# A row sum over 67 MB: blocks of 16 rows in place of 8, rows shared evenly between two engines, and a last block cut 8, 5, 2 and a split row

## The chip, the cores and the metric

The kernel runs on one core of a Trainium2 chip. The metric is device time in microseconds (us) of one execution; the time before is the median of 13 runs, 164.68 us (164.46 to 165.12).

## The reference

```
batch, seq, dim = 32, 512, 1024          # x: float32
def reference(x, multiplier):            # multiplier = 0.5
    return (np.sum(x, axis=-1) * multiplier).astype(np.float32)
```

Each of 16,384 rows of 1024 numbers is summed and multiplied by 0.5. 67.1 MB are read and 64 KiB written.

## The kernel before

The rows are laid over the 128 partitions so that partition p has rows 128 p to 128 p + 127, one after another in memory. So each partition has 128 rows of 4 KiB, and a load of c rows for all partitions moves 128 contiguous pieces of c x 4 KiB.

Fifteen big blocks (lines 74 to 91) of 8 rows each are loaded into a pool of three buffers (line 76; 4 MiB a load, in pieces of 32 KiB). VectorE sums 7 of the 8 rows with one reduce (line 78) and multiplies the 7 sums (line 83). ScalarE does the eighth with an activation that copies, scales and accumulates (line 53, called from line 90); it writes its scaled copy over the row, and a second small instruction reads the accumulator out.

The last 8 rows of each partition, the taper (lines 93 to 103), are loaded in six pieces of 2, 2, 1, 1, 1 and 1 rows, into buffers of their own (line 97). ScalarE does the first five rows; VectorE does the last three with `tensor_tensor_reduce` (line 62), which adds the two halves of a row to each other and accumulates, so that 1024 numbers take 512 steps. It too is followed by a small accumulator read.

All loads and the one store at the end (line 106) are issued by SP, in program order. A load into a buffer that is used again waits until both engines have done with it and until the load before it landed. The taper's loads don't wait for a buffer. The store waits for the last results of both engines. The names in the profile are `x_tile_b` for the big blocks, `x_tile_s` for the taper, `staging` for unscaled sums and `out_sbuf` for results.

Of the kernel before, what the change touches and what calls it, by code (L numbers as in the profile page):

```python
# [1 line left out]

# [4 lines left out]


@with_exitstack  # L10
def kernel(
    ctx: ExitStack,
    tc: tile.TileContext,
    x: bass.AP,
    multiplier: float,
    out: bass.AP,
):
    nc = tc.nc
    P = nc.NUM_PARTITIONS
    fp32 = mybir.dt.float32  # L20

    x_flat = x.flatten_outer_dims()
    N, D = x_flat.shape
    H = D // 2
    out_flat = out.rearrange("b s -> (b s)")

    assert N % P == 0
    rows_per_part = N // P

    taper = [(2, "s"), (2, "s"), (1, "s"), (1, "v"), (1, "v"), (1, "v")]  # L30
    taper_rows = sum(sz for sz, _ in taper)
    big_rows = 8
    assert (rows_per_part - taper_rows) % big_rows == 0
    n_big = (rows_per_part - taper_rows) // big_rows

    scalar_rows_per_big = 1
    vec_rows_per_big = big_rows - scalar_rows_per_big

    x_rows = x_flat.rearrange("(p c) d -> p c d", p=P)
    out_view = out_flat.rearrange("(p c) -> p c", p=P)  # L40

    big_pool = ctx.enter_context(tc.tile_pool(name="big", bufs=3))
    small_pool = ctx.enter_context(tc.tile_pool(name="small", bufs=4))
    res_pool = ctx.enter_context(tc.tile_pool(name="res", bufs=1))
    small_bufs = {2: 2, 1: 4}

    staging = res_pool.tile([P, rows_per_part], fp32)
    out_sbuf = res_pool.tile([P, rows_per_part], fp32)

    mul = float(multiplier)  # L50

    def scalar_row_sum(x_tile, r, col):
        nc.scalar.activation(  # L53
            out=x_tile[:, r, :],
            in_=x_tile[:, r, :],
            func=mybir.ActivationFunctionType.Copy,
            scale=mul,
            accum_out=out_sbuf[:, col : col + 1],
        )

    def vector_row_sum(x_tile, r, col):
        nc.vector.tensor_tensor_reduce(  # L62
            out=x_tile[:, r, 0:H],
            in0=x_tile[:, r, 0:H],
            in1=x_tile[:, r, H:D],
            scale=mul,
            scalar=0.0,
            op0=mybir.AluOpType.add,
            op1=mybir.AluOpType.add,
            accum_out=out_sbuf[:, col : col + 1],  # L70
        )

    c0 = 0
    for _ in range(n_big):
        x_tile = big_pool.tile([P, big_rows, D], fp32, name="x_tile_b")
        nc.sync.dma_start(out=x_tile, in_=x_rows[:, c0 : c0 + big_rows, :])  # L76

        nc.vector.reduce_sum(  # L78
            out=staging[:, c0 : c0 + vec_rows_per_big],
            in_=x_tile[:, 0:vec_rows_per_big, :],  # L80
            axis=mybir.AxisListType.X,
        )
        nc.vector.tensor_single_scalar(  # L83
            out=out_sbuf[:, c0 : c0 + vec_rows_per_big],
            in_=staging[:, c0 : c0 + vec_rows_per_big],
            scalar=mul,
            op=mybir.AluOpType.mult,
        )
        for r in range(vec_rows_per_big, big_rows):
            scalar_row_sum(x_tile, r, c0 + r)  # L90
        c0 += big_rows

    for sz, eng in taper:
        x_tile = small_pool.tile(
            [P, sz, D], fp32, name=f"x_tile_s{sz}", tag=f"s{sz}", bufs=small_bufs[sz]
        )
        nc.sync.dma_start(out=x_tile, in_=x_rows[:, c0 : c0 + sz, :])  # L97
        for r in range(sz):
            if eng == "s":
                scalar_row_sum(x_tile, r, c0 + r)  # L100
            else:
                vector_row_sum(x_tile, r, c0 + r)
        c0 += sz
    assert c0 == rows_per_part

    nc.sync.dma_start(out=out_view, in_=out_sbuf)


# [1 line left out]
_INS = ['x', 'multiplier']  # L110
_OUTS = [((32, 512), 'float32')]
#: Inputs that are plain numbers.
_NUMBERS = {'multiplier': 0.5}


# [26 lines left out]
```

## Time and profile before

| | |
|---|---|
| Median of 13 runs | 164.68 us |
| Profiled execution, its own time | 164.63 us |
| Its span, first to last instruction | 162.6 us |
| VectorE (DVE) busy | 118.9 us, 73% |
| ScalarE (ACT) busy | 23.9 us, 15% |
| DMA queue, share of 16 engines' span | 96.7% |
| Mean rate over the span | 413 GB/s |
| Big load, from issue to landing | 21.4 us (median) |
| Reduce of 7 rows (L78) | 7.62 us, 15 times |
| ScalarE row (L53) | 1.06 us, and 0.19 for the accumulator |
| VectorE row in the taper (L62) | 0.69 us, and 0.08 for the accumulator |

The profile is of one execution. DVE is VectorE, ACT ScalarE, SPq the queue of SP, which issues the DMAs. In the timeline a row gives start, duration, engine, line and operation, then what is written and read, and in brackets the idle time of the engine before it and what ended that. The row of 40 slices gives tenths of busy share; in the table of stretches each row has the busy time of VectorE, ScalarE and GpSimd, then the granted clock of TensorE, the share of the DMA engines' time and the rate.

### The profile page before, as it was taken

How to read it: one execution, taken by the hardware profiler on the slowest of the kernel's cores; microseconds unless marked ns; L12 is line 12 of the kernel's file. 1: busy time of each engine (PE TensorE's matmuls, PEld its weight loads, DVE VectorE, ACT ScalarE, POOL GpSimd, SP SyncE). 2: the span in 40 equal slices, each digit the busy share in tenths (PEclk: the TensorE clock that was granted, in tenths of full speed). 3: DMA queues.
4: the chain of work that ended last, by engine and by line, in shares of the span. 5: the costliest groups of instructions: out<-in, count | busy, mean ns of one | idle time of the engine just before them, and what ended most of it. 6: DMA issues, size and time to landing. Idle time of an engine off the chain costs nothing.

```text
span 162.6 us, 170 instructions
## 1 busy us (share of the span) xinstructions
DVE 118.9 (73%) x36; ACT 23.9 (15%) x41; POOL 0.2 (0%) x4
## 2 busy tenths in 40 slices
DVE  0007959599595977959599695968959598695982
ACT  3002020020201102020020202002020020202670
POOL 0000000000000000000000000000000000000000
DMA  6999999999999999999999999999999999998990
GB/s 210 435 403 451 435 443 411 435 443 435 411 443 435 411 459 443 395 459 435 403 451 435 435 419 435 443 427 419 443 435 411 443 435 411 451 443 365 411 389 20
DMA packets 3168, 67.18 MB, mean 413 GB/s; under 512 B 352, under 2 KB 480, under 8 KB 992
## 3 DMA queue, kind: packets, MB, share of 16 engines
q1 hardware_dynamic: 3168, 67.18, 96.7%
HBM read 67.11 MB, written 0.07 MB: 413 GB/s over the span
## 4 chain that ended last, share of the span: by engine, by line
DMA 76%; DVE 19%; SPq 2%; issue 0%; DVEq 0%
DMA x_tile_b<-in_x_dram 59%; DVE staging L78 19%; DMA x_tile_s<-in_x_dram 18%; SPq L97 1%; SPq L76 1%; DVE x_tile_s L62 0%; DVEq L137 0%
## 5 line engine op out<-in xcount | busy, mean ns | idle before, releaser
L78 DVE TENSOR_REDUCE staging<-x_tile_b 128x7 f32<-128x7168 f32 x15 | 114.3, 7619 | 39.8 <-DMA x_tile_b<-in_x_dram 39.8
L53 ACT ACTIVATE x_tile_b<-x_tile_b 128x1024 f32<-128x1024 f32 x15 | 15.8, 1057 | 131.3 <-DMA x_tile_b<-in_x_dram 131.3
L53 ACT ACTIVATE x_tile_s<-x_tile_s 128x1024 f32<-128x1024 f32 x5 | 5.2, 1047 | 1.6 <-DMA x_tile_s<-in_x_dram 1.6
L83 DVE TENSOR_SCALAR out_sbuf<-staging 128x7 f32<-128x7 f32 x15 | 2.6, 171 | 0.5
L53 ACT ACTIVATION_READ_ACCUMULATOR x_tile_b<-x_tile_b 128x1 f32 x15 | 2.8, 186 | 0.0
L62 DVE CUSTOM_DVE_ANT_0 x_tile_s<-x_tile_s 128x512 f32<-128x512 f32 x3 | 2.1, 690 | 0.9 <-DMA x_tile_s<-in_x_dram 0.9
L53 ACT ACT_TABLE_LOAD x1 | 1.3, 1283 | 0.7 <-PEq L123 0.7
L53 ACT ACTIVATION_READ_ACCUMULATOR x_tile_s<-x_tile_s 128x1 f32 x5 | 0.9, 187 | 0.0
L62 DVE DVE_READ_ACCUMULATOR2_ANT out_sbuf<- 128x1 f32 x3 | 0.2, 82 | 0.0
L123 POOL MEMSET const-bfloat16-1.0<- 128x1 bf16 x1 | 0.1, 102 | 0.0
L123 POOL MEMSET const-uint8-127<- 128x1 uint8 x1 | 0.1, 101 | 0.0
L123 POOL MEMSET const-float32-0.0<- 128x1 f32 x1 | 0.1, 99 | 0.2 <-issue 0.2
L123 POOL MEMSET const-float32-1.0<- 128x1 f32 x1 | 0.1, 98 | 0.0
## 6 DMA issues: line engine op xcount, KB each, us to landing
x_tile_b<-in_x_dram SPq DMA_DIRECT2D x15, 4096.0 KB, 21.4
x_tile_s<-in_x_dram SPq DMA_DIRECT2D x2, 1024.0 KB, 24.6
x_tile_s<-in_x_dram SPq DMA_DIRECT2D x4, 512.0 KB, 27.6
out_dram<-out_sbuf SPq DMA_DIRECT2D x1, 64.0 KB, 1.5
```

Of the source, the lines that this page charges most:

```text
L53: nc.scalar.activation(out=x_tile[:, r, :], in_=x_tile[:, r, :], func=mybir.ActivationFunctionType.Copy, scale=mul, accum_out=out_sbuf[:, ...
L62: nc.vector.tensor_tensor_reduce(out=x_tile[:, r, 0:H], in0=x_tile[:, r, 0:H], in1=x_tile[:, r, H:D], scale=mul, scalar=0.0, op0=mybir.Alu ...
L76: nc.sync.dma_start(out=x_tile, in_=x_rows[:, c0 : c0 + big_rows, :])
L78: nc.vector.reduce_sum(out=staging[:, c0 : c0 + vec_rows_per_big], in_=x_tile[:, 0:vec_rows_per_big, :], axis=mybir.AxisListType.X,)
L83: nc.vector.tensor_single_scalar(out=out_sbuf[:, c0 : c0 + vec_rows_per_big], in_=staging[:, c0 : c0 + vec_rows_per_big], scalar=mul, op=m ...
L97: nc.sync.dma_start(out=x_tile, in_=x_rows[:, c0 : c0 + sz, :])
L123: nc = _bacc.Bacc("TRN2", target_bir_lowering=False, num_devices=1)
```

## The change

The loop now goes over blocks of 16 rows: seven of them in one load each (8 MiB, in contiguous pieces of 64 KiB), three buffers as before. VectorE reduces and scales rows 0 to 7, ScalarE does rows 8 to 15. The eighth block is loaded into one buffer of the same pool in five loads: rows 0 to 7, rows 8 to 12, rows 13 and 14, then columns 0 to 639 of row 15, then its columns 640 to 1023. There ScalarE does rows 4 to 7, 11, 12 and 14; VectorE does the others a row at a time by adding halves. The last row takes two VectorE instructions: the first leaves a scaled sum of 640 columns in `part`, the second starts its accumulation from `part` and adds the 384 others. SP issues 13 DMAs in place of 22. The instructions that scale and sum are of the same kinds as before. Line numbers in the changed kernel: big load 71, reduce 73, multiply 76, ScalarE row 47, VectorE row 57, the last block's loads 90 and 92, store 104.

```diff
-    taper = [(2, "s"), (2, "s"), (1, "s"), (1, "v"), (1, "v"), (1, "v")]
-    big_rows = 8
-    big_pool = ctx.enter_context(tc.tile_pool(name="big", bufs=3))
-    small_pool = ctx.enter_context(tc.tile_pool(name="small", bufs=4))
+    B = 16
+    x_pool = ctx.enter_context(tc.tile_pool(name="x", bufs=3))
+    part = res_pool.tile([P, 1], fp32, name="part")
...
+    def dve_span(t, r, lo, hi, dst, start=0.0):
+        mid = (lo + hi) // 2
+        nc.vector.tensor_tensor_reduce(
+            out=t[:, r, lo:mid],
+            in0=t[:, r, lo:mid],
+            in1=t[:, r, mid:hi],
+            scale=mul,
+            scalar=start,
+            op0=ADD,
+            op1=ADD,
+            accum_out=dst,
+        )
...
-    for _ in range(n_big):
-        x_tile = big_pool.tile([P, big_rows, D], fp32, name="x_tile_b")
-        nc.sync.dma_start(out=x_tile, in_=x_rows[:, c0 : c0 + big_rows, :])
+    for b in range(n_blocks - 1):
+        c0 = b * B
+        t = x_pool.tile([P, B, D], fp32, name="xb")
+        nc.sync.dma_start(out=t, in_=x_rows[:, c0 : c0 + B, :])
+        h = B // 2
         nc.vector.reduce_sum(
+            out=sums[:, c0 : c0 + h], in_=t[:, 0:h, :], axis=mybir.AxisListType.X
         )
...
+        for r in range(h, B):
+            act_row(t, r, c0 + r)
...
-    for sz, eng in taper:
...
-        nc.sync.dma_start(out=x_tile, in_=x_rows[:, c0 : c0 + sz, :])
+    c0 = (n_blocks - 1) * B
+    t = x_pool.tile([P, B, D], fp32, name="xb")
+    cut = 640
+    pieces = [(0, 8), (8, 13), (13, 15)]
+    for lo, hi in pieces:
+        nc.sync.dma_start(out=t[:, lo:hi, :], in_=x_rows[:, c0 + lo : c0 + hi, :])
+    for lo, hi in ((0, cut), (cut, D)):
+        nc.sync.dma_start(
+            out=t[:, B - 1, lo:hi], in_=x_rows[:, c0 + B - 1, lo:hi]
+        )
+    on_act = {4, 5, 6, 7, 11, 12, 14}
+    for r in range(B - 1):
+        if r in on_act:
+            act_row(t, r, c0 + r)
+        else:
+            dve_span(t, r, 0, D, res[:, c0 + r : c0 + r + 1])
+    dve_span(t, B - 1, 0, cut, part)
+    dve_span(t, B - 1, cut, D, res[:, rows - 1 : rows], start=part)
```

More of the change, by code (lines that the diff above doesn't have):

```diff
@@ L5 @@
 import concourse.tile as tile
-from concourse import bass_utils, mybir
+from concourse import mybir
 from concourse._compat import with_exitstack
@@ L20 @@
     fp32 = mybir.dt.float32
+    ADD = mybir.AluOpType.add
     x_flat = x.flatten_outer_dims()
     N, D = x_flat.shape
[L24 to L28, printed above, removed]
-    taper = [(2, "s"), (2, "s"), (1, "s"), (1, "v"), (1, "v"), (1, "v")]
-    taper_rows = sum(sz for sz, _ in taper)
-    big_rows = 8
-    assert (rows_per_part - taper_rows) % big_rows == 0
-    n_big = (rows_per_part - taper_rows) // big_rows
-    scalar_rows_per_big = 1
@@ L37 @@
-    vec_rows_per_big = big_rows - scalar_rows_per_big
-    x_rows = x_flat.rearrange("(p c) d -> p c d", p=P)
-    out_view = out_flat.rearrange("(p c) -> p c", p=P)
-    big_pool = ctx.enter_context(tc.tile_pool(name="big", bufs=3))
-    small_pool = ctx.enter_context(tc.tile_pool(name="small", bufs=4))
-    res_pool = ctx.enter_context(tc.tile_pool(name="res", bufs=1))
-    small_bufs = {2: 2, 1: 4}
-    staging = res_pool.tile([P, rows_per_part], fp32)
-    out_sbuf = res_pool.tile([P, rows_per_part], fp32)
@@ L50 @@
-    mul = float(multiplier)
-    def scalar_row_sum(x_tile, r, col):
+    rows = N // P
+    x_rows = x_flat.rearrange("(p c) d -> p c d", p=P)
+    out_view = out.rearrange("b s -> (b s)").rearrange("(p c) -> p c", p=P)
+    mul = float(multiplier)
+    B = 16
+    n_blocks = rows // B
+    assert N == P * rows and rows == n_blocks * B
+    x_pool = ctx.enter_context(tc.tile_pool(name="x", bufs=3))
+    res_pool = ctx.enter_context(tc.tile_pool(name="res", bufs=1))
+    sums = res_pool.tile([P, rows], fp32, name="sums")
@@ L53, in scalar_row_sum, with act_row @@
+    res = res_pool.tile([P, rows], fp32, name="res")
+    part = res_pool.tile([P, 1], fp32, name="part")
+    def act_row(t, r, col):
         nc.scalar.activation(
-            out=x_tile[:, r, :],
-            in_=x_tile[:, r, :],
+            out=t[:, r, :],
+            in_=t[:, r, :],
             func=mybir.ActivationFunctionType.Copy,
             scale=mul,
-            accum_out=out_sbuf[:, col : col + 1],
+            accum_out=res[:, col : col + 1],
         )
-    def vector_row_sum(x_tile, r, col):
+    def dve_span(t, r, lo, hi, dst, start=0.0):
+        mid = (lo + hi) // 2
@@ L62, in vector_row_sum @@
         nc.vector.tensor_tensor_reduce(
-            out=x_tile[:, r, 0:H],
-            in0=x_tile[:, r, 0:H],
-            in1=x_tile[:, r, H:D],
+            out=t[:, r, lo:mid],
+            in0=t[:, r, lo:mid],
+            in1=t[:, r, mid:hi],
             scale=mul,
[L67 to L70, printed above, removed]
-        )
-    c0 = 0
-    for _ in range(n_big):
-        x_tile = big_pool.tile([P, big_rows, D], fp32, name="x_tile_b")
-        nc.sync.dma_start(out=x_tile, in_=x_rows[:, c0 : c0 + big_rows, :])
+            scalar=start,
@@ L78 @@
+            op0=ADD,
+            op1=ADD,
+            accum_out=dst,
+        )
+    for b in range(n_blocks - 1):
[3 more added lines that the diff above has]
+        h = B // 2
         nc.vector.reduce_sum(
-            out=staging[:, c0 : c0 + vec_rows_per_big],
-            in_=x_tile[:, 0:vec_rows_per_big, :],
-            axis=mybir.AxisListType.X,
+            out=sums[:, c0 : c0 + h], in_=t[:, 0:h, :], axis=mybir.AxisListType.X
@@ L82 @@
         )
         nc.vector.tensor_single_scalar(
-            out=out_sbuf[:, c0 : c0 + vec_rows_per_big],
-            in_=staging[:, c0 : c0 + vec_rows_per_big],
+            out=res[:, c0 : c0 + h],
+            in_=sums[:, c0 : c0 + h],
             scalar=mul,
@@ L88 @@
         )
-        for r in range(vec_rows_per_big, big_rows):
-            scalar_row_sum(x_tile, r, c0 + r)
-        c0 += big_rows
-    for sz, eng in taper:
-        x_tile = small_pool.tile(
-            [P, sz, D], fp32, name=f"x_tile_s{sz}", tag=f"s{sz}", bufs=small_bufs[sz]
-        )
-        nc.sync.dma_start(out=x_tile, in_=x_rows[:, c0 : c0 + sz, :])
[L98 to L106, printed above, removed]
+        for r in range(h, B):
[9 more added lines that the diff above has]
+            out=t[:, B - 1, lo:hi], in_=x_rows[:, c0 + B - 1, lo:hi]
+        )
+    on_act = {4, 5, 6, 7, 11, 12, 14}
[6 more added lines that the diff above has]
+    dve_span(t, B - 1, cut, D, res[:, rows - 1 : rows], start=part)
+    nc.sync.dma_start(out=out_view, in_=res)
 _INS = ['x', 'multiplier']
```

## The prediction

> **What bounds the kernel now.** I read the page first (engine shares, the 40 slices, the chain), then the engines by stretches, then the SP queue's waits, then the timeline, mostly its end. From the page:
>
> ```profile
> DVE 118.9 (73%) x36; ACT 23.9 (15%) x41; POOL 0.2 (0%) x4
> DMA  6999999999999999999999999999999999998990
> q1 hardware_dynamic: 3168, 67.18, 96.7%
> DMA 76%; DVE 19%; SPq 2%; issue 0%; DVEq 0%
> ```
>
> The second row is the mean busy share of the 16 DMA engines: nines from the second slice to the last but two. No compute engine is near that. The chain gives VectorE 19%, which looks like a compute bound; the stretches (us from:to, length, engines' busy us, granted clock, DMA share, GB/s) and the SP queue's waits say otherwise:
>
> ```profile
> 32.00:62.00 30.00, 23.49 (x7) 3.49 (x7) 0.00 (x0) 1.00 1.01 434
> ...
> 130.00:150.00 20.00, 16.14 (x5) 2.85 (x5) 0.00 (x0) 1.00 0.98 421
> 150.00:158.00 8.00, 7.69 (x4) 5.94 (x12) 0.00 (x0) 1.00 1.00 408
> 158.00:160.00 2.00, 1.35 (x4) 0.00 (x0) 0.00 (x0) 1.00 0.20 78
> ```
> ```profile
> SPq L76 <- DVE staging L78: 121.5, 12, 18.9
> ```
>
> The DMA share is 0.98 to 1.01 up to 158 us. SP does wait for VectorE to free a buffer (twelve times, 121.5 us), but each time the rest of one load (1.9 us of it) and a whole further one are still queued, so the DMA engines never run dry. VectorE's 19% of the chain is how the chain is followed back through a wait that costs nothing. So the time is: start, 67.1 MB streamed without a gap, and what follows the last landing. The timeline has all three parts (start us, us, engine and line; engines start 0.02 us after a landing, so starts in which the engine had been idle are landings):
>
> ```profile
> 13.32 7.62 DVE L78 TENSOR_REDUCE staging<-x_tile_b 128x7 f32<-128x7168 f32 x1 [13.32 <-DMA x_tile_b<-in_x_dram]
> ...
> 149.30 7.62 DVE L78 TENSOR_REDUCE staging<-x_tile_b 128x7 f32<-128x7168 f32 x1 [1.90 <-DMA x_tile_b<-in_x_dram]
> ...
> 151.78 1.06 ACT L53 ACTIVATE x_tile_s<-x_tile_s 128x1024 f32<-128x1024 f32 x1 [1.25 <-DMA x_tile_s<-in_x_dram]
> ...
> 154.28 1.06 ACT L53 ACTIVATE x_tile_s<-x_tile_s 128x1024 f32<-128x1024 f32 x1 [0.31 <-DMA x_tile_s<-in_x_dram]
> ...
> 156.95 0.17 DVE L83 TENSOR_SCALAR out_sbuf<-staging 128x7 f32<-128x7 f32 x1
> ...
> 159.35 0.69 DVE L62 CUSTOM_DVE_ANT_0 x_tile_s<-x_tile_s 128x512 f32<-128x512 f32 x1 [0.53 <-DMA x_tile_s<-in_x_dram]
> 159.97 0.08 DVE L62 DVE_READ_ACCUMULATOR2_ANT out_sbuf<- 128x1 f32 x1
> 160.12 0.35 SPq L106 DMA_DIRECT2D out_dram<-out_sbuf  x1
> ```
>
> First landing at 13.30, last at 159.33; then one row on VectorE (0.69), the store's issue at 160.12, the end at 162.6. The profiled execution took 164.63, so 2.03 lies around its span; it stands 0.05 below the median of 164.68.
>
> **The stream: what a row of each length costs.** A load of 128 rows gives each of 16 engines 8 rows. Spacing of landings by row length: 32 KiB rows (4 MiB), (149.30 - 13.32)/14 = 9.713 us; 8 KiB rows (1 MiB), 2.48 and 2.50; 4 KiB rows (512 KiB), (159.35 - 154.28)/4 = 1.268. A line through the first and last: (9.713 - 1.268)/28 = 0.3016 us per KiB of row, and 1.268 - 4 x 0.3016 = 0.061 us fixed per load of eight rows an engine, some 8 ns a row. At 8 KiB it gives 2.474 against 2.49 seen, so it holds inside its span. 64 KiB lies outside it.
>
> Loads of 16 rows replace two of 8. By the line one takes 0.061 + 64 x 0.3016 = 19.365 against 2 x 9.713 = 19.426: 0.061 saved, times 7 = 0.43 us. Bounds: nothing, if a 64 KiB row goes as two of 32 KiB; a loss, if it is cut finer (below). No row shows a 64 KiB transfer. The Trainium skill, "DMA: Bandwidth & Descriptors", section "Why a DMA increments its semaphore by 16 and not by 1", says that one descriptor moves one contiguous run, and speaks of cutting only for rows longer than 64 KiB; 64 KiB is just not longer. I take 0.43.
>
> The last 8 rows of each partition: before 2 x 2.49 + 4 x 1.268 = 10.05 us (six loads). After, loads of 5 rows (20 KiB: 0.061 + 6.032 = 6.093), 2 rows (2.49), 640 columns (2.5 KiB: 0.815) and 384 columns (1.5 KiB: 0.513), 9.91 us in sum; the 8 rows before them are one load of 32 KiB rows as now. Saved 0.14. The last landing moves from 159.33 by 0.43 + 0.14 to 158.76.
>
> A rule speaks against those pieces. The same page, section "Anatomy of one DMA", gives each DMA of GpSimd's path about 2.0 us plus bytes/436e9. Read as a time per load in a row, the 320 and 192 KiB pieces would take 2.75 and 2.45 us in place of 0.815 and 0.513: 3.9 us later. The trace's own row for the nearest size (512 KiB, SP's queue) is 1.268 us of spacing, against 3.2 by the rule: with loads queued, the fixed part lies under the transfer before it. I take the row. For the same reason nine loads fewer (22 DMAs to 13) don't save nine times 2.0 us.
>
> **After the last landing.** Now: 0.69 us of VectorE. For shorter pieces I have 7168 elements in 7.619 us and 7 in 0.171: 1.040 ns an element and 0.164 fixed, which gives 0.696 for 512 against 0.693 seen. The 640-column piece (320 elements) then takes 0.497 and the last (192) 0.364. Sequence: the 2-row piece lands at 157.43; row 13 runs on VectorE 157.45 to 158.14. The 640 columns land at 158.25, run 158.27 to 158.77. The last columns land at 158.76; their instruction takes the partial sum as its start value, so it waits also for VectorE's own result: the nearest row is the multiply behind each reduce, which follows it by 0.03. Start 158.81, end 159.17, store issued 0.07 later at 159.24 instead of 160.12. Bounds of that new wait: none (0.03 less), or some 0.1 more if the per-partition start value is slow to read; only the store queues behind it. ScalarE's row 14 runs 157.45 to 158.7 (1.06 and 0.19), inside VectorE's time. The store is unchanged.
>
> **What is moved and hidden.** Per block VectorE gets 8 rows: 0.164 + 8192 x 1.040 = 8.68 plus 0.17; ScalarE 8 rows at 1.06 = 8.5 plus 0.19, against 1 before. Both lie in a block's 19.4 us. The block before the last lands 9.71 us before the 8-row piece, so both engines are through (8.9) just before they get it; if that cover were gone, the 8-row piece's four rows each (4.2 us) would still end before the 5-row piece, 6.1 later. These rows cost nothing. Buffers: the fourth load waits for block 0's release, about 9 us after it landed, with 10.5 us of one load and a whole one still queued; the last block's five issues (about 0.43 each, by the tail's present issues) stand some 30 us before their data's turn. SP queues nothing else behind them but the store. Would ScalarE's 63 rows slow the loads? In 150 to 158 ScalarE is busy 74% and the DMA share stays 1.00; its 408 GB/s is the short rows. I take nothing; a per-mille of the stream (0.15) is a fair upper bound. The start: issue and first transfer are unchanged, and no engine has been near late since.
>
> Sum on the profiled execution: 0.43 + 0.14 + (159.35 + 0.69 - 159.33) less (159.17 - 158.76), that is 0.57 + 0.71 - 0.41 = 0.87, near the 0.88 of the store's issue; 164.63 - 0.88 = 163.75, on the median 163.8.
>
> **Rivals.** *64 KiB rows go as two of 32 KiB.* Then 0.43 comes back: 164.24, say 164.2. For: 32 KiB is the longest row shown. Against: the page's words. *Rows are cut finer (slower).* Place: each of seven big loads; price: cut into 4 KiB, 16 x 1.268 - 19.426 = 0.86 each, 6.0 in all, so 170.2. Cut into 16 KiB, 4 x (0.061 + 16 x 0.3016) = 19.55, 0.12 each, 0.87 in all: 165.1; against the remaining 0.45 of gain it decides from pieces of 16 KiB downwards. Against: the page's count, 3168 packets, leaves 2176 once those under 8 KiB (992) are off; 15 x 128 rows of 32 KiB plus 2 x 128 of 8 KiB is 2176. So rows to 32 KiB are not cut. *Small last loads pay their fixed time*: 163.8 + 3.9 = 167.7. *Part of the end is given back* (a slow start value, a few tenths of disturbance by ScalarE's traffic or by a longer program): 164.1 to 164.4.
>
> **How the numbers follow.** Forecast 0.60 (163.5 to 164.1). Two of 32 KiB 0.17. Given back 0.15, half of it within 0.2% of now. Finer cut 0.05, fixed time at the end 0.03. A change within 0.2% (0.33 us, so above 164.35) can't be told from none. Faster: 0.60 + 0.17 + about 0.08 = 0.85; same 0.07; slower 0.08. The range reaches to the two-of-32 case and part of what is given back: 163.4 to 164.5.
>
> **What would show it.** Spacing of block landings: 19.37 (right), 19.43 (two of 32 KiB), above 19.5 (cut finer). Packets: 7 x 128 + 128 x 5 for the loads, plus semaphores and store, if 64 KiB goes as one. Landings of the last pieces 0.8 and 0.5 us apart; the last VectorE instruction 0.36 us, starting within 0.06 of the last landing; store issue near 159.24. The prediction is wrong if the DMA share falls under 1.00 between blocks, if the last VectorE instruction starts long after its data, or if the stream slows while ScalarE works.

## The result, and the profile after

The changed kernel takes 163.92 us (median of 11 runs, 163.66 to 164.35) against 164.63 us before (49 runs): a ratio of 0.9955, 95% interval 0.9946 to 0.9964. Forecast were 163.8 us and a range of 163.4 to 164.5. The sum holds; the terms behind it hold only in part. The profiled execution took 163.94 us with a span of 162.155 us; before, 164.63 and 162.601.

From the page of the changed kernel, the rows shown of before and the new row of the queue that loads programs:

```profile
DVE 68.1 (42%) x34; ACT 67.9 (42%) x127; POOL 0.2 (0%) x4
DMA  7979979969979979979999998998998997999990
DMA packets 1874, 67.18 MB, mean 414 GB/s; under 512 B 209, under 2 KB 465, under 8 KB 593
q1 hardware_dynamic: 1872, 67.18, 96.4%
q14 instruction: 2, 0.01, 0.0%
DMA 85%; DVE 11%; SPq 1%; issue 0%; DVEq 0%
```

1872 packets are 896 of 64 KiB (seven loads of 128 rows), 640 for the five last loads, 208 semaphore writes and 128 of the store: a 64 KiB row goes as one. In the packet records one takes 2418 ns, and one of 32 KiB 1213 to 1214. The views count a packet whole where it begins, so with packets of 2.4 us the digits of slices of 4.05 us swing (`7979`), and the shares of stretches with them:

```profile
32.00:62.00 30.00, 8.95 (x3) 8.52 (x17) 0.00 (x0) 1.00 1.00 433
...
120.00:140.00 20.00, 9.45 (x3) 8.94 (x17) 0.00 (x0) 1.00 0.96 415
140.00:150.00 10.00, 9.02 (x5) 8.70 (x17) 0.00 (x0) 1.00 0.97 419
150.00:158.00 8.00, 3.98 (x13) 5.95 (x13) 0.00 (x0) 1.00 0.96 402
158.00:160.00 2.00, 1.35 (x6) 0.88 (x2) 0.00 (x0) 1.00 0.05 18
```

From 120 to 158 us the rows show 0.96 and 0.97, and the prediction named a share under 1.00 as a sign of being wrong. With every packet cut at the edges of the stretch, the packet records give 1.00 for the first two and at least 0.99 for the third: the DMA engines stay busy, as before.

SP's wait for a buffer is there four times in place of twelve for the big loads, and again costs nothing:

```profile
SPq L71 <- DVE sums L73: 86.8, 4, 29.6
```

The timeline, first blocks and end (a reduce starts 0.02 to 0.03 behind its block's landing):

```profile
22.96 8.69 DVE L73 TENSOR_REDUCE sums<-xb 128x8 f32<-128x8192 f32 x1 [22.96 <-DMA xb<-in_x_dram]
...
42.54 8.69 DVE L73 TENSOR_REDUCE sums<-xb 128x8 f32<-128x8192 f32 x1 [10.69 <-DMA xb<-in_x_dram]
...
139.41 8.69 DVE L73 TENSOR_REDUCE sums<-xb 128x8 f32<-128x8192 f32 x1 [10.46 <-DMA xb<-in_x_dram]
...
157.73 0.69 DVE L57 CUSTOM_DVE_ANT_0 xb<-xb 128x512 f32<-128x512 f32 x1 [0.57 <-DMA xb<-in_x_dram]
...
158.52 0.49 DVE L57 CUSTOM_DVE_ANT_0 xb<-xb 128x320 f32<-128x320 f32 x1
...
158.94 0.08 DVE L57 DVE_READ_ACCUMULATOR2_ANT part<- 128x1 f32 x1
159.10 0.42 DVE L57 CUSTOM_DVE_ANT_0 xb<-xb,part 128x192 f32<-128x192 f32 x1
...
159.60 0.35 SPq L104 DMA_DIRECT2D out_dram<-res  x1
```

The first block lands at 22.93, as the prediction's line has it (13.30 + 9.71 - 0.06 = 22.95). The next reduce starts at 42.54: 19.58 for the second block, where 19.37 was forecast. The last data lands at 158.97 by the trace's landing records, the last instruction starts 0.13 later, and takes 0.42 where 0.36 was reckoned. The store is issued at 159.60, not at 159.24. So the span alone gives 0.45 us of the forecast 0.88. What makes up for it lies outside the span: 164.63 - 162.60 = 2.03 us before, 163.94 - 162.155 = 1.78 now. That was in no step of the prediction.

### The profile page after: what moved, and what is told of

Read it like the earlier page. It is cut to its first block, busy times and chain, and to the rows that moved or that the text cites. A ratio compares the mean times of both kernels' runs of the same rounds, so it can differ in the third digit from the quotient of the medians.

```text
span 162.2 us, 233 instructions
## 1 busy us (share of the span) xinstructions
DVE 68.1 (42%) x34; ACT 67.9 (42%) x127; POOL 0.2 (0%) x4
## 3 DMA queue, kind: packets, MB, share of 16 engines
q1 hardware_dynamic: 1872, 67.18, 96.4%
## 4 chain that ended last, share of the span: by engine, by line
DMA 85%; DVE 11%; SPq 1%; issue 0%; DVEq 0%
DMA xb<-in_x_dram 85%; DVE sums L73 11%; SPq L90 1%; DVE xb L57 1%; SPq L71 0%; DVE part L57 0%; DVEq L135 0%
## 5 line engine op out<-in xcount | busy, mean ns | idle before, releaser
L47 ACT ACTIVATE xb<-xb 128x1024 f32<-128x1024 f32 x63 | 65.6, 1043 | 90.3 <-DMA xb<-in_x_dram 90.3
L73 DVE TENSOR_REDUCE sums<-xb 128x8 f32<-128x8192 f32 x7 | 60.8, 8686 | 86.1 <-DMA xb<-in_x_dram 86.1
L47 ACT ACTIVATION_READ_ACCUMULATOR xb<-xb 128x1 f32 x63 | 11.8, 188 | 0.0
L57 DVE CUSTOM_DVE_ANT_0 xb<-xb 128x512 f32<-128x512 f32 (+1 forms) x9 | 5.6, 667 | 5.1 <-DMA xb<-in_x_dram 5.0
L76 DVE TENSOR_SCALAR res<-sums 128x8 f32<-128x8 f32 x7 | 1.2, 171 | 0.2
L57 DVE DVE_READ_ACCUMULATOR2_ANT res<- 128x1 f32 x9 | 0.7, 82 | 0.0
```

The lines of the kernel that those rows point to most:

```text
L47: nc.scalar.activation(out=t[:, r, :], in_=t[:, r, :], func=mybir.ActivationFunctionType.Copy, scale=mul, accum_out=res[:, col : col + 1],)
L57: nc.vector.tensor_tensor_reduce(out=t[:, r, lo:mid], in0=t[:, r, lo:mid], in1=t[:, r, mid:hi], scale=mul, scalar=start, op0=ADD, op1=ADD, ...
L73: nc.vector.reduce_sum(out=sums[:, c0 : c0 + h], in_=t[:, 0:h, :], axis=mybir.AxisListType.X)
L76: nc.vector.tensor_single_scalar(out=res[:, c0 : c0 + h], in_=sums[:, c0 : c0 + h], scalar=mul, op=mybir.AluOpType.mult,)
```

## The experiments

My theory at this point: the stream's gain is the fixed 8 ns of a row, halved in number, less what a disturbance took; the new end's gain is the shorter last instruction less a wait. The rivals: all of the gain is in the end; all of it is in the stream. "Landing" below is by the landing records; "around" is an execution's time less its span. For executions other than the profiled one the span is on record to 0.1 us only, so a single "around" of theirs is good to 0.05.

**Half of the change: the big blocks alone.**

```diff
-    pieces = [(0, 8), (8, 13), (13, 15)]
+    pieces = [(0, 8), (8, 10), (10, 12), (12, 13), (13, 14), (14, 15), (15, 16)]
...
-    for lo, hi in ((0, cut), (cut, D)):
-        nc.sync.dma_start(
-            out=t[:, B - 1, lo:hi], in_=x_rows[:, c0 + B - 1, lo:hi]
-        )
-    on_act = {4, 5, 6, 7, 11, 12, 14}
+    on_act = {4, 5, 6, 7, 8, 9, 10, 11, 12}
...
-    dve_span(t, B - 1, 0, cut, part)
-    dve_span(t, B - 1, cut, D, res[:, rows - 1 : rows], start=part)
+    dve_span(t, B - 1, 0, D, res[:, rows - 1 : rows])
```

> Half of the change: seven loads of 64 KiB rows, rows shared 8 and 8, but the last 8 rows in six loads (2, 2, 1, 1, 1, 1) and the last row whole, as before. My theory (the rows' fixed 8 ns is the gain of the stream, 0.43 us, of which a disturbance and one program fetch took back up to 0.3): block landings 19.35 to 19.37 us apart, time 164.2 to 164.5. Rival (all of the gain is in the end; the stream gains nothing net): 164.6, as before. Rival (the stream is the whole gain and the new end gives nothing): 163.9.

Measured: 164.01 us (163.82 to 164.07), ratio 0.9954 (0.9941 to 0.9968). The end of its timeline:

```profile
158.87 0.69 DVE L57 CUSTOM_DVE_ANT_0 xb<-xb 128x512 f32<-128x512 f32 x1 [0.52 <-DMA xb<-in_x_dram]
...
159.63 0.35 SPq L99 DMA_DIRECT2D out_dram<-res  x1
```

Blocks land 19.33 to 19.36 us apart, but for one of 19.43. The last landing is at 158.84 (0.49 before that of the kernel before), the time around the span is 1.77. The time is 0.2 below the theory's interval: the big blocks bring nearly all of the gain, and 0.25 of it is around the span, where the theory had nothing.

**The other half: the new end alone.** Fourteen blocks of 8 rows from a pool of three, then the last block of the change.

```diff
-    x_pool = ctx.enter_context(tc.tile_pool(name="x", bufs=3))
+    x_pool = ctx.enter_context(tc.tile_pool(name="x", bufs=1))
+    s_pool = ctx.enter_context(tc.tile_pool(name="s", bufs=3))
...
-    for b in range(n_blocks - 1):
-        c0 = b * B
-        t = x_pool.tile([P, B, D], fp32, name="xb")
-        nc.sync.dma_start(out=t, in_=x_rows[:, c0 : c0 + B, :])
-        h = B // 2
+    S = 8
+    for b in range((rows - B) // S):
+        c0 = b * S
+        t = s_pool.tile([P, S, D], fp32, name="x8")
+        nc.sync.dma_start(out=t, in_=x_rows[:, c0 : c0 + S, :])
+        h = S - 1
...
-        for r in range(h, B):
+        for r in range(h, S):
```

> The other half: fourteen blocks of 8 rows, shared 7 and 1 as before, then the new last block (8, 5, 2, 640 and 384 columns). My theory: 0.14 us from the last rows' transfers and some 0.14 from the shorter last instruction (0.55 from the last landing to its end in place of 0.69 and 0.02), so 164.3 to 164.4, landings 9.71 apart, no program fetch within the span. Rival (all gain is in the end): 163.9. Rival (the stream is the whole gain): 164.6.

Measured: 164.74 us (164.48 to 165.26), ratio 1.0008 (0.9996 to 1.0019): no gain at all, against 0.3 expected. Its end:

```profile
158.82 0.49 DVE L58 CUSTOM_DVE_ANT_0 xb<-xb 128x320 f32<-128x320 f32 x1
...
159.38 0.42 DVE L58 CUSTOM_DVE_ANT_0 xb<-xb,part 128x192 f32<-128x192 f32 x1
...
159.87 0.35 SPq L106 DMA_DIRECT2D out_dram<-res  x1
```

The last rows' transfers did get shorter: 9.87 us from the last 8-row landing to the last of all, 10.05 before. Three things eat that. The first block landed 0.10 later (13.40; in the kernels with 8-row loads it lands between 13.30 and 13.44). From the last landing to the store's issue it is 0.63 in place of 0.79, but from there to the end of the span 2.63 in place of 2.48. And 2.20 us lie around the span, not 2.03. The last two have nothing to do with how the last rows are summed, and became the questions of the later runs.

**Only the length of a row: the same blocks in two loads.**

```diff
-        nc.sync.dma_start(out=t, in_=x_rows[:, c0 : c0 + B, :])
+        for q in range(0, B, 8):
+            nc.sync.dma_start(
+                out=t[:, q : q + 8, :], in_=x_rows[:, c0 + q : c0 + q + 8, :]
+            )
```

> The changed kernel, but each block of 16 rows comes in two loads of 8 rows (rows of 32 KiB) into the same buffer: only the length of a row in a load changes. My theory: 0.061 us more for each of seven blocks, landings 19.42 apart, time 0.43 more than the changed kernel, 164.3. Rival (the length of the row is nothing): 163.9. If the slow packets at 27 to 30 us belong to 64 KiB rows, they are gone here, and the difference is 0.2.

Measured: 164.37 us (164.24 to 164.88), 0.45 above the changed kernel's 163.92. From its timeline, three reduces:

```profile
71.65 8.69 DVE L76 TENSOR_REDUCE sums<-xb 128x8 f32<-128x8192 f32 x1 [10.53 <-DMA xb<-in_x_dram]
91.36 8.69 DVE L76 TENSOR_REDUCE sums<-xb 128x8 f32<-128x8192 f32 x1 [10.82 <-DMA xb<-in_x_dram]
110.78 8.69 DVE L76 TENSOR_REDUCE sums<-xb 128x8 f32<-128x8192 f32 x1 [10.53 <-DMA xb<-in_x_dram]
```

16 rows take 19.42 (91.36 to 110.78), where one load takes 19.35: the 0.06 to 0.07 a block is the length of the row. The packet records have it too: two rows of 32 KiB (1213 to 1214 ns each) take some 9 ns more than one of 64 KiB (2418), and each engine has eight such pairs in a block, 0.07 us. Not all of the 0.45 belongs to the rows, though: this kernel issues 20 DMAs in place of 13, which by the last experiment below costs some 0.06 at the end of the program. That leaves about 0.39 for the rows. From 71.65 to 91.36 it is 19.71: here the packet records have an 8 KiB program fetch at 85.34 us, on the queue that the page calls q14, and the next landing came 0.28 late. One such packet takes 309 ns on one of the 16 engines. It delays the next landing in some executions and not in others; why is not shown.

**Sharing the rows.**

```diff
-        h = B // 2
+        h = B - 1
```

> The changed kernel with VectorE on 15 and ScalarE on 1 row of each of the seven blocks, so 49 ScalarE rows fewer and a shorter ScalarE program; VectorE needs 0.164 + 15360 x 1.040 ns = 16.1 us of 19.35 for a block. My theory (even sharing gives nothing, and the longer ScalarE program costs a fetch of 8 KiB in the middle of the stream, 0.09 us): no fetch within the span, and a time 0.1 less or equal, 163.8 to 163.9. Rival (ScalarE's writes slow the stream, the slow packets at 27 to 30 us): those slow packets are gone and it is 0.2 to 0.3 faster, 163.6. Rival (sharing the rows is needed): slower than the changed kernel, 164.2 or more.

Measured: 165.54 us, ratio 1.0051 (1.0036 to 1.0065), slower than before. Its timeline from the last big block on:

```profile
139.18 16.15 DVE L73 TENSOR_REDUCE sums<-xb 128x15 f32<-128x15360 f32 x1 [2.99 <-DMA xb<-in_x_dram]
155.25 0.68 DVE L57 CUSTOM_DVE_ANT_0 xb<-xb 128x512 f32<-128x512 f32 x1
...
160.64 0.08 DVE L57 DVE_READ_ACCUMULATOR2_ANT part<- 128x1 f32 x1
160.75 0.42 DVE L57 CUSTOM_DVE_ANT_0 xb<-xb,part 128x192 f32<-128x192 f32 x1
...
161.25 0.35 SPq L104 DMA_DIRECT2D out_dram<-res  x1
```

The last big reduce runs to 155.3, while the next 8 rows have been there since 148.9; VectorE then works off eight rows and a split one back to back (no idle time in brackets) until 161.17, 2.4 us behind the last landing at 158.75. I had compared 16.1 us with a block's 19.35, but behind the last big block only 9.7 pass to the next piece. My theory that sharing gives nothing falls; the prediction's paragraph had it right with its 8.9 of 9.71. The stream itself is undisturbed, with landings 19.34 to 19.36 apart, and no program fetch.

**The changed kernel again.** No edit.

> The changed kernel once more, to see which of its losses come back: the slow packets at 27 to 30 us (0.22 us on the second block's landing) and the program fetch of 8 KiB at 85 us (0.09). My theory: the fetch comes back at the same place, since it belongs to ScalarE's program; the slow packets don't, and blocks 2 to 7 all land 19.35 to 19.45 apart. Rival: both belong to the kernel and come back. Time 163.8 to 164.0.

Measured: 163.82 us (163.65 to 163.94), ratio 0.9944 (0.9931 to 0.9958). Three of its reduces:

```profile
23.25 8.69 DVE L73 TENSOR_REDUCE sums<-xb 128x8 f32<-128x8192 f32 x1 [23.25 <-DMA xb<-in_x_dram]
42.59 8.69 DVE L73 TENSOR_REDUCE sums<-xb 128x8 f32<-128x8192 f32 x1 [10.44 <-DMA xb<-in_x_dram]
...
139.34 8.69 DVE L73 TENSOR_REDUCE sums<-xb 128x8 f32<-128x8192 f32 x1 [10.46 <-DMA xb<-in_x_dram]
```

Six blocks in 116.09 us, 19.35 each; 116.45 in the first profile. The slow packets of 27 to 30 us are gone, so they do not come in every execution of this kernel. The program fetch is there again (87.1 us), this time without a cost. This execution lost 0.3 at its start instead (23.25 for 22.96).

**The last row in one piece.**

```diff
-    pieces = [(0, 8), (8, 13), (13, 15)]
+    pieces = [(0, 8), (8, 13), (13, 15), (15, 16)]
...
-    for lo, hi in ((0, cut), (cut, D)):
-        nc.sync.dma_start(
-            out=t[:, B - 1, lo:hi], in_=x_rows[:, c0 + B - 1, lo:hi]
-        )
...
-    dve_span(t, B - 1, 0, cut, part)
-    dve_span(t, B - 1, cut, D, res[:, rows - 1 : rows], start=part)
+    dve_span(t, B - 1, 0, D, res[:, rows - 1 : rows])
```

> The changed kernel with the last row in one load of 4 KiB rows and one VectorE instruction: loads 8, 5, 2, 1 rows. My theory: the last loads take 1.27 us in place of 1.26 (0.79 and 0.47), so the last landing stays within 0.05; the last instruction is 0.69 from 0.02 behind it in place of 0.42 from 0.13 behind it: 0.16 us later, time 164.0 to 164.1. Rival (the split's whole reckoned gain of 0.33 is there): 164.25. Rival (the wait and the start value eat the split's gain): 163.9.

Measured: 164.11 us (163.92 to 164.32), 0.29 above the changed kernel of the same chip's runs. Its end:

```profile
158.99 0.69 DVE L57 CUSTOM_DVE_ANT_0 xb<-xb 128x512 f32<-128x512 f32 x1 [0.53 <-DMA xb<-in_x_dram]
...
159.77 0.35 SPq L99 DMA_DIRECT2D out_dram<-res  x1
```

From the last landing (158.97) to the store 0.80, against 0.63 with the split: the split is worth 0.16, as the theory has it. Another 0.07 of the 0.29 is behind the store (2.63 in place of 2.55). The 0.06 left is within the scatter of five executions each. The profiled one also had slow packets, again at 27 to 30 us: its first blocks lay 19.49 and 19.54 apart.

**Another cut.**

```diff
-    cut = 640
+    cut = 576
```

> The changed kernel with the last row cut at 576 in place of 640 columns. My theory (the last instruction waits for the partial sum, 0.13 behind the last landing, not for its data): the second piece lands 0.55 behind the first, the first piece's instruction takes 0.46, so the partial sum is ready at about the last landing; the last instruction (224 elements) takes 0.45 and starts 0.03 to 0.06 behind the landing; the store is issued 0.04 to 0.07 earlier. In time 163.85, hardly told from 163.92. Rival (the start is late for another reason): it starts 0.13 behind the landing as before, and the store 0.03 later.

Measured: 164.04 us (163.69 to 164.09), ratio 0.9954 (0.9940 to 0.9967), not to be told from the changed kernel's 0.9944 (0.9931 to 0.9958) of the same chip's runs. The trace can tell:

```profile
158.55 0.08 DVE L57 DVE_READ_ACCUMULATOR2_ANT part<- 128x1 f32 x1
158.82 0.45 DVE L57 CUSTOM_DVE_ANT_0 xb<-xb,part 128x224 f32<-128x224 f32 x1 [0.19 <-DMA xb<-in_x_dram]
...
159.36 0.35 SPq L104 DMA_DIRECT2D out_dram<-res  x1
```

The partial sum is read out by 158.63, the data lands at 158.69, and still the instruction starts at 158.82, 0.13 behind the landing as with 640. My explanation (it waits for the partial sum) falls, the rival holds: landing to store 0.67 in place of 0.63.

**No start value.**

```diff
-    dve_span(t, B - 1, cut, D, res[:, rows - 1 : rows], start=part)
+    dve_span(t, B - 1, cut, D, res[:, rows - 1 : rows])
```

> The changed kernel, but the last instruction starts from zero in place of the partial sum: the last row's result leaves out its first 640 columns. It shows the price of the start value and of the wait for it. My theory: the instruction takes 0.36 us in place of 0.42, and starts 0.02 to 0.08 earlier; store issue 0.1 earlier. Rival (0.42 is simply what 192 elements take): still 0.42.

Measured in a single execution: 163.76 us.

```profile
158.95 0.08 DVE L57 DVE_READ_ACCUMULATOR2_ANT part<- 128x1 f32 x1
158.99 0.36 DVE L57 CUSTOM_DVE_ANT_0 xb<-xb 128x192 f32<-128x192 f32 x1
...
159.43 0.35 SPq L104 DMA_DIRECT2D out_dram<-res  x1
```

Landing at 158.96, start at 158.99, 0.36 long. So the start value costs 0.06 within the instruction and 0.11 ahead of it. In the changed kernel's trace a semaphore instruction of VectorE stands in that gap (158.99 to 159.02), and here there is none: the instruction with the start value waits for two things, for the landing in that separate instruction and for VectorE's own result in itself. The pair costs the 0.11, but only when the landing has just come. In all eight profiles with a start value in which it had, the last instruction starts 0.13 to 0.14 behind the landing, whether the partial sum was ready 0.05 to 0.06 before it or 0.05 to 0.08 behind it. In the ninth, with rows shared 15 and 1, the landing was two microseconds old and its semaphore instruction done (158.78); there the partial sum is read out at 160.72 and the last instruction starts at 160.75, the 0.03 that the prediction took.

**Around the span: fewer ScalarE rows in the kernel before.** In the first profiles 1.78 us lay around the span of every kernel but two: before (2.03) and the new end alone (2.20). Those two have 20 and 21 ScalarE rows, the others 14, or 63 and more.

```diff
-    for _ in range(n_big):
+    for i in range(n_big):
+        vec_rows = big_rows if i < 7 else vec_rows_per_big
...
-            out=staging[:, c0 : c0 + vec_rows_per_big],
-            in_=x_tile[:, 0:vec_rows_per_big, :],
+            out=staging[:, c0 : c0 + vec_rows],
+            in_=x_tile[:, 0:vec_rows, :],
...
-            out=out_sbuf[:, c0 : c0 + vec_rows_per_big],
-            in_=staging[:, c0 : c0 + vec_rows_per_big],
+            out=out_sbuf[:, c0 : c0 + vec_rows],
+            in_=staging[:, c0 : c0 + vec_rows],
...
-        for r in range(vec_rows_per_big, big_rows):
+        for r in range(vec_rows, big_rows):
```

> The kernel before, but VectorE does all 8 rows of the first seven big blocks (8.69 us of 9.71), so ScalarE has 13 rows in place of 20. Nothing on the path changes within the span. So far the time around the span was 1.78 us in every kernel whose ScalarE had 14 or 63 rows, 2.03 and 2.20 where it had 20 and 21, and in those two the trace has a program fetch of 8 KiB behind the last instruction. My theory (the length of ScalarE's program decides where its next 8 KiB are fetched: within the stream when it is long, at the very end when it has 20 rows, never when it is shorter): around the span 1.78, span 162.6 as before, time 164.4, without a fetch. Rival (something else of the 8-row kernels, the SP program or the number of loads): 2.03 and 164.65, as before.

Measured: 164.50 us (164.36 to 164.68), ratio 0.9991 (0.9982 to 0.9999). Its page has the fewer ScalarE instructions, and nothing else of note:

```profile
DVE 126.3 (78%) x36; ACT 15.9 (10%) x27; POOL 0.2 (0%) x4
```

Around the span 1.78 in the profiled execution and 1.75 to 1.83 in all eleven (mean 1.79). The kernel before had 1.82 to 2.15 in 17 executions beside it (mean 2.00). The span is no shorter (162.73, its first block being 0.14 later). So seven ScalarE rows of 128 are worth about 0.2 us in a place where no busy row shows them.

**21 and 15 ScalarE rows in the changed kernel.** The cut is 576 in both; only the last big block is shared.

```diff
-        h = B // 2
+        h = B // 2 if b == n_blocks - 2 else B - 1
...
-    cut = 640
+    cut = 576
```

> The changed kernel with the cut at 576, and VectorE on 15 and ScalarE on 1 row in blocks 0 to 5, 8 and 8 in block 6 alone: ScalarE has 21 rows. My theory (sharing is needed only in the last big block, which has 9.7 us and not 19.4 until the next piece lands): store issue near 159.35 as with the cut at 576 and 8 and 8 rows throughout, not 161.25; and around the span 2.0 to 2.2, since 21 rows put the program fetch at the end, so 163.9 to 164.1. Rival for the end (sharing is needed throughout): store issue later than 160. Rival for the time around the span (it belongs to the 8-row kernels): 1.78, 163.65.

Measured: 163.93 us (163.74 to 164.23), around the span 1.93, less than the 2.0 to 2.2 expected, but away from 1.78 in all five executions (1.93 to 1.97). The profiled execution, at 164.23 the slowest of them, has blocks that landed late:

```profile
42.42 16.15 DVE L73 TENSOR_REDUCE sums<-xb 128x15 f32<-128x15360 f32 x1 [3.01 <-DMA xb<-in_x_dram]
62.03 16.15 DVE L73 TENSOR_REDUCE sums<-xb 128x15 f32<-128x15360 f32 x1 [3.25 <-DMA xb<-in_x_dram]
81.48 16.15 DVE L73 TENSOR_REDUCE sums<-xb 128x15 f32<-128x15360 f32 x1 [3.08 <-DMA xb<-in_x_dram]
```

19.61 and 19.45: slow packets, with ScalarE nearly idle. So these are not ScalarE's doing. A program fetch behind the last instruction, which the theory wanted, is not among this profile's packet records. The store was issued 0.67 behind the last landing, as with rows shared throughout: sharing is needed in the last big block only.

With `B` in place of `B - 1` ScalarE has 15 rows:

> The same with all 16 rows of blocks 0 to 5 on VectorE (17.2 us of 19.35 for a block): ScalarE has 15 rows. My theory: no program fetch in the span nor behind it, around the span 1.78, block landings 19.35 throughout, store issue 159.3, time 163.6 to 163.7: 0.2 to 0.3 less than the changed kernel, and 0.3 less than with 21 rows. If the slow packets of some 64 KiB profiles come from ScalarE's writes, there are none here. Rival (six ScalarE rows are nothing): the same time as with 21 rows.

Measured: 163.88 us (163.63 to 164.19), around the span 1.78, and in the profiled execution (163.72) all blocks 19.33 to 19.36 apart, with no row of the program queue in the page. The trace is as expected, the median is not: 0.05 below the 21 rows, inside the scatter of both. In time this pair tells nothing apart.

**The end of the program.** In the traces SP waits, behind the store, once for each of the completion semaphores that the DMAs take in turn, and the waits that stand behind the store's own come after its landing, 0.06 us each.

```diff
+    pad = res_pool.tile([P, 3], fp32, name="pad")
...
+        if b == 2:
+            for q in range(3):
+                nc.sync.dma_start(out=pad[0:16, q : q + 1], in_=x_rows[0:16, q, 0:1])
```

> The kernel with 15 ScalarE rows and the cut at 576, plus three loads of one number to each of 16 partitions, which nobody uses, issued behind the second big load's issue: 16 DMAs in place of 13. The DMAs take eight completion semaphores in turn, and at the program's end SP waits for each in turn, 0.062 us each; those before the store's own are done while the store is on its way. From the store's issue to the end of the span the runs so far took 2.42 us with 15 DMAs, 2.48 with 22, 2.55 with 13, 2.61 to 2.63 with 12 and 20: the fewer lanes come behind the store's, the shorter. My theory: with 16 DMAs the store has the last lane, and the end takes 2.55 - 3 x 0.062 = 2.37 us; the span, undisturbed, is 161.75 in place of 161.94, the time 163.65 to 163.7. Rival (the end differs for another reason, such as the store's own landing): 2.55, and 163.88.

Measured: 163.71 us (163.59 to 163.80), ratio 0.9941 (0.9928 to 0.9955), the fastest of all, though not clearly ahead of the changed kernel's second set (163.82). (The three loads stand behind the third big load, not the second: `b` counts from 0.)

```profile
159.04 0.45 DVE L58 CUSTOM_DVE_ANT_0 xb<-xb,part 128x224 f32<-128x224 f32 x1 [0.20 <-DMA xb<-in_x_dram]
...
159.57 0.35 SPq L108 DMA_DIRECT2D out_dram<-res  x1
```

The span ends at 161.93, 2.36 behind the store's issue; 2.37 was expected, and the same kernel without the three loads took 2.57. From the store's landing to the end of the span:

| DMAs | place of the store's semaphore among eight | landing to end, us |
|---|---|---|
| 16 (this) | 8th | 0.81 |
| 15 (big blocks alone) | 7th | 0.88 |
| 22 (before; 13 ScalarE rows) | 6th | 0.94, 0.94 |
| 13 (changed) | 5th | 1.00 |
| 12 (last row whole), 20 (new end alone, two loads) | 4th | 1.06, 1.06, 1.05 |

## Why the prediction came out

Its time is right, its sum is only half right, and that 163.8 and 163.92 lie so near each other is luck: half of what the span fell short of was made up for by a term that the prediction did not have. By the two profiled executions, in us:

| Term | forecast | measured |
|---|---|---|
| Stream, to the last landing | -0.57 | -0.36 (again: -0.45) |
| Last landing to store's issue | -0.31 | -0.16 |
| Store's issue to end of span | 0 | +0.07 |
| Around the span | 0 | -0.24 |
| Sum | -0.88 | -0.69 |

*The fixed time of a row* was right: 19.355 us for an undisturbed block against 19.365, and about 0.39 us of time against 0.43 when the length of the row is undone (0.45, less the 0.06 for the store's place). That a 64 KiB row goes as one packet was right (2418 ns), and the two rivals on cutting fell.

*The last rows' transfers*: right, 19.58 from the last big block to the end against 19.62. Small last loads pay no fixed time: 0.79 and 0.47 apart, so that rival fell too.

*"The start: issue and first transfer are unchanged, and no engine has been near late since"*: too smooth. The stream's 0.21 shortfall is 0.22 of slow packets in that execution and 0.09 of a program fetch, less 0.10 gained in small parts. The fetch is shown as the cost of ScalarE's 63 rows: it is there, at 85 to 88 us, in all seven profiles with so many rows and in none of those with 21 or fewer. Its price is 0 to 0.28. The prediction named a longer program only among what might be given back. Slow packets were also in four of the nine other profiles of 64 KiB rows, in parts of up to 0.3. In the first profile and in one of these four (the last row whole) they came at 27 to 30 us, while ScalarE worked; in the other three they came mostly while it was idle. So they need no work of ScalarE's. What causes them stays open. So does whether 64 KiB rows have more of them: in the four profiles of 32 KiB rows no block is late but for the program fetch, which is few to go by, and the kernel before scatters as much in time (164.27 to 165.3).

*"Start 158.81, end 159.17"*: the step that failed by most of its size. The new wait was taken as 0.03 from the nearest row, a wait for one thing. An instruction that waits for a fresh landing and for its own engine starts 0.13 behind the landing, not 0.05 as forecast, and the start value adds 0.06. Half of the split's gain went there. A slow start value was among the bounds (0.1 more); that the wait itself could cost more than 0.03 was not.

*"The store is unchanged"*: its issue and landing are (1.55 and 1.54), what follows is not. One place lower in the turn of semaphores costs 0.06.

*Around the span*: not foreseen. With ScalarE's 20 rows some 0.2 us more lie around the span than with 63; the change happened to move away from that count. That this goes with ScalarE's row count is shown, in the kernel before by itself. The mechanism is argued only: in two of the kernels concerned (before and the new end alone) the packet records have an 8 KiB program fetch behind the last instruction, but not with 21 rows and the cut at 576 (1.93).

Without the last of these terms the time would have been about 164.2, still inside the range. The new end, a good half of the diff, brings 0.1 to 0.2 us behind 16-row blocks (163.92 and 163.82 against 164.01) and nothing behind 8-row ones, where the end of the program and the time around the span took it back. Some 0.4 comes from 64 KiB rows, and some 0.2 goes with ScalarE's count of rows.

## What to carry to other kernels

When the DMA engines are busy throughout, count what is fixed per row of a load and per instruction behind the last landing, and give every extra wait its own price: here an instruction that waited for a landing alone, or for its own engine's result with the landing long past, started 0.02 to 0.03 us behind it, and one that needed both started 0.13 to 0.14 behind a fresh landing. Compare an engine's time for a block with the time until the next piece, not with the time of a block: a taper behind big blocks changes that. And in a change of a few tenths, read the time around the span as well as the span: how many rows ScalarE has, and how many DMAs come before the last, moved the time here by up to 0.2 us each, of a gain of 0.7.

## What the runs showed of the hardware that was not expected

Whether 8 KiB of program are fetched in mid-stream goes with ScalarE's count of rows: once, at 85 to 88 us, with 63 or 65 rows (309 ns on one of 16 DMA engines, 0 to 0.28 us on a landing), never with 21 or fewer. With 20 or 21 the time around the span of the profiled executions is 1.93 to 2.20 instead of 1.78. An instruction of VectorE that needs a landing and its own engine's result starts 0.13 to 0.14 us behind a landing that has just come, and 0.03 behind the result when the landing is old. Three loads of 16 numbers each, which nobody uses, made the end of the program 0.19 us shorter by giving the store the last of eight semaphores.
